# A state-space layer rewritten as a table of ticks, with every engine and the SP queue in program order

## The chip, the core and the metric

One core of a Trainium2 chip runs the kernel. The core has five instruction streams that matter here: PE (TensorE, matrix products), ACT (ScalarE, functions of one input), DVE (VectorE, element-wise work), POOL (GpSimd, element-wise work) and SP (SyncE, which here only issues DMAs). Each stream is executed in its own order, and streams wait for each other through semaphores. The metric is the device time of one execution in microseconds (us), lower is better.

## The reference

The function is one decode and prefill step of a two-layer model: a state-space layer (Mamba-2 style, "SSD") and then a latent-attention layer ("MLA"). Only the SSD layer is touched. Cut to what matters:

```python
def ssd_mixer(h, conv_buf, ssm_state, w_in, conv_w, conv_b, dt_bias, a_log, d_skip, norm_w, w_out):
    proj = jnp.einsum('btd,de->bte', h, w_in)
    z, xbc, dt_raw = ...                                  # gates, inputs of the convolution, steps
    xbc, new_buf = causal_conv(xbc, conv_buf, conv_w, conv_b)
    xbc = jax.nn.silu(xbc)                                # x (32 heads x 64), B and C (8 groups x 128)
    dt = jax.nn.softplus(dt_raw + dt_bias)
    y, new_state = ssd_scan(x, dt, -jnp.exp(a_log), B, C, ssm_state)
    y = (y + d_skip * x) * jax.nn.silu(z)
    yg = y per group of 256 channels
    y = yg * lax.rsqrt(mean(yg * yg) + eps) * norm_w
    out = jnp.einsum('bte,ed->btd', y, w_out)
```

There are 1024 prompt tokens and 8 sample sequences of 8 tokens, 1088 rows in all. The scan works on chunks of 128 tokens. With `a` the running sum of the decays in a chunk, one chunk needs M = exp(a_l - a_s) * (C B^T) below the diagonal, y = M (x dt) + exp(a) C S, and the state S = fade * S + (x dt decay)^T B. The samples start from states in memory, and return new ones.

## The kernel before

**Precision and tiling.** A product in full precision is done as three products of halves: every factor is split into a rounded part (hi) and the rest (lo), and `mm3` or `mm_tok` add hi*hi, hi*lo and lo*hi in one PSUM bank. A split (`split`, L127) is a copy on ACT (hi) and a subtraction on DVE or POOL (lo). The 1088 rows are nine tiles, the last one (64 rows) is the samples.

**Groups.** The layer goes through eight groups of four heads. A group has two parts. The *projections* (class `Group`): four blocks of 128 channels (B, C, and two of x), each in three column pieces of 384, 384 and 320 tokens (products named pj, 24 a piece); each piece is copied out of PSUM by ACT into `raw`, then the convolution is one ACT operation and three DVE operations (`acc`, L468) of 1112 columns; and nine tiles of gates (products named pz, 24 a tile). The weights come in pieces of 256 KB (`wraw`, L272), which ACT and DVE split into `wih` and `wil`. The *scan* (`ssd_scan`): for each of nine tiles PE transposes x and B (trp), makes C B^T (cb), the product within the chunk (py), the state's increment (st) and the product with the state (py from Sh, Sl); DVE, ACT and POOL make what these need. The ninth tile is the samples: four pieces of old state (s) are loaded, transposed (s0p), split (sh, sl), used (pv) and renewed (sn, s).

**What sets the order.** The code is written as generators: the loop over groups in `layer_ssd` runs the projections of group g+1 beside the scan of group g, by weights, and a scheduler then orders each engine's instructions by its own model, so neighbours in the code need not be neighbours on an engine. The scheduler also pulls weights of group 1 ahead into the time of group 0 (seven 256 KB pieces).

**Ahead of the loop** stand group 0's projections and `ssd_dt` (L335), which turns the step sizes into decays: ACT, DVE and PE work on `dtu`, `acs`, `acsp`, and then SP writes the decays to memory (`acs_d`, L387) and copies `tok` (L376, six small DMAs). The scan reads `acs_d` back once for each chunk (M, L573).

**After the loop** comes the output projection, in two halves of eight input blocks (`ssd_outproj`, products poa and pob): `load_wout` loads and splits w_out (woh L703, wol L704), each tile of y is read back, scaled, transposed (ytp), split and multiplied. The first half runs beside the scan of group 7. The MLA layer follows.

The change and the prediction touch L575 (four DVE operations a chunk that make min(a_l - a_s, 0) for M), L577 (exp on ACT), L578 (times C B^T), L656 to L664 (y, the gate, the square for the norm, the multiplication by the norm weight nw on POOL, the store), L477 (co: the last three columns of the convolution on their way out, from the PSUM bank ctp), L129 and L130 (the two halves of a split) and L429 (silu of the convolution).

Of the kernel before, what the change touches and what calls it, by code (L numbers as in the profile page):

```python
# [8 lines left out]
F32 = mybir.dt.float32  # L9
# [7 lines left out]
D = 1024  # L17
# [62 lines left out]
PB1 = {"tr": 2, "pj": 2, "cb": 1, "y": 2, "st": 1}  # L80
# [254 lines left out]
def ssd_dt(k, pool, psum):  # L335
# [19 lines left out]
    pt = psum.tile([128, 512], F32, tag="y", name="dpt", bufs=PB["y"])  # L355
# [50 lines left out]
class Group:  # L406
# [10 lines left out]
    def pair(self, pi, both=False):  # L417
# [3 lines left out]
        if both:  # L421
            for _ in range(3):
# [6 lines left out]
        nc.scalar.activation(acc[:, :, :SEQ], acc[:, :, :SEQ], AF.Silu)  # L429
        nc.scalar.activation(xs.rearrange("p a (b w) -> p a b w", w=NT),  # L430
                             bass_window(acc, SEQ + 3, NT + 3, NT), AF.Silu)
        self.xc.append((acc, xs))
        if pi:
            self.conv_out()
# [53 lines left out]
    def gates(self):  # L488
# [4 lines left out]
        for i, (t0, m) in enumerate(TILES):  # L493
# [15 lines left out]
            if i == 4:  # L509
                nc.scalar.activation(z, z, AF.Silu)  # L510
            yield
# [9 lines left out]
def ssd_scan(k, gr, pools):  # L521
    nc, I = k.nc, k.I
    sp, psum = pools
    g = gr.g
    S = None
    hs = slice(4 * g, 4 * g + 4)
    nw = sp.tile([128, 256], F32, tag="nw", name=f"nw{g}", bufs=1)
    nc.sync.dma_start(nw, I["ssd_norm_w"][0, 256 * g : 256 * g + 256].partition_broadcast(128))
    for i in ORDER[g]:
        t0, m = TILES[i]  # L530
        sl = slice(t0, t0 + m)
        smp = i == 8
        B, C, X0, X1 = (gr.xc[q][1][:, j] if smp else gr.xc[q][0][:, j, sl] for q in range(2) for j in range(2))
        z = gr.z[i // 5][:m, i % 5]
        tag = f"{g}_{i}"
        p = psum.tile([128, 512], F32, tag="tr", name="trp" + tag, bufs=PB["tr"])
        nc.tensor.transpose(p[:m, 0:128], X0, k.ident)
        nc.tensor.transpose(p[:m, 128:256], X1, k.ident)
        if not smp:
            nc.tensor.transpose(p[:m, 256:384], B, k.ident)  # L540
        xsT = sp.tile([128, 256], F32, tag="xsT", name="xsT" + tag, bufs=2)
        nc.scalar.copy(xsT[:m], p[:m, 0:256])
        if not smp:
            Bh, Bl = (sp.tile([128, 128], F32R, tag="BT" + x, name="BT" + x + tag, bufs=2) for x in "hl")
            split(k, Bh, Bl, p[:, 256:384])
        tk = k.tok[:m, i]

        def hb(j):
            return tk[:, j, hs].unsqueeze(2).to_broadcast([m, 4, 64])

        def v3(t):
            return t[:m].rearrange("p (h q) -> p h q", q=64)

        xdt = sp.tile([128, 256], F32, tag="xdt", name="xdt" + tag, bufs=2)
        nc.vector.tensor_tensor(v3(xdt), v3(p[:, 0:256]), hb(1), op=ALU.mult)  # L555
        if not smp:
            xdd = sp.tile([128, 256], F32, tag="xdd", name="xdd" + tag, bufs=1)
            nc.gpsimd.tensor_tensor(v3(xdd), v3(xsT), hb(2), op=ALU.mult)
            dh, dl = (sp.tile([128, 256], F32R, tag="xdd" + x, name="xdd" + x + tag, bufs=1) for x in "hl")
            split(k, dh, dl, xdd, nc.gpsimd)  # L560
            if S is not None:
                Ch, Cl = (sp.tile([128, 128], F32R, tag="C" + x, name="C" + x + tag, bufs=1) for x in "hl")
                split(k, Ch, Cl, C, nc.gpsimd)
                Sh, Sl = (sp.tile([128, 256], F32R, tag="S" + x, name="S" + x + tag, bufs=1) for x in "hl")
                split(k, Sh, Sl, S, nc.gpsimd)
# [30 lines left out]
        else:  # L596
# [7 lines left out]
            for q in range(2):  # L604
# [20 lines left out]
                for pr in range(2):  # L625
# [4 lines left out]
                    for b in range(4):  # L630
                        nc.tensor.transpose(pt[:, b * 128 : b * 128 + 128], s0[:, b], k.ident)
# [1261 lines left out]
```

## Time and profile before

| | us |
|---|---|
| time, median of 3 runs | 2100.28 (2096.88 to 2101.25) |
| the profiled execution, first to last instruction (its span) | 2095.4 |
| loop over groups 1 to 7 (first pj of group 1 to last pz), from 116.7 | 730.9 |
| rest of the scan and first half of the output projection | 169.0 |
| second half of the output projection | 106.9 |
| MLA layer, from 1123.5 | 971.9 |

The profile has no time of its own for the profiled execution beside its span; the median run is 4.9 us longer than that span, which is what lies around it.

A page of the profile lists the busy time of each engine, then groups of instructions (line, engine, operation, written tile <- read tiles, count, busy time, mean of one, idle time ahead of it and what ended that). The view by windows gives for one stretch of time: start and end, length, then busy time and count of PE, PE's weight loads, DVE, ACT and POOL, then the clock that PE was granted (1.00 is full), the share of the DMA engines and GB/s. The timeline gives start, duration, engine, line, operation, tiles and, in brackets, how long the engine had been idle and for whom.

### The profile page before, as it was taken

Reading aid. Unit: us, or ns where it says so; the run is one execution under the profiler, and the core shown is the slowest. Engines: PE = TensorE matmul, PEld = TensorE weight load, DVE = VectorE, ACT = ScalarE, POOL = GpSimd, SP = SyncE. Lnnn points to the kernel's source line nnn. Section 1 sums busy time; section 2 is a strip of 40 time slices with the busy share of each in tenths; the row PEclk is TensorE's granted clock in tenths of the full one; section 3 lists DMA queues with packets and bytes.
Section 4 is the critical chain, followed back from the end, with each engine's and each line's share of the span. In section 5 each row is a group of like instructions: output and inputs, shape, how many; then the busy total and the mean of one; then the engine's idle time right before and its main releaser. Section 6 shows DMA issues by size and latency. Waiting matters only on the chain.

```text
span 2095.4 us, 33766 instructions
## 1 busy us (share of the span) xinstructions
PE 1948.3 (93%) x12001; PEld 1763.6 (84%) x12001; DVE 1340.1 (64%) x2838; ACT 1043.3 (50%) x2287; POOL 851.9 (41%) x1059
## 2 busy tenths in 40 slices
PE   6999999999999999789998999699999999889998
PEld 5898999899999998677787998698888888778887
DVE  4558676767676767865334314366787778776665
ACT  5455565556565656522114323234676667755552
POOL 0337564646664646744000001102343334765541
PEclk9999999999999999889999999899999989999999
DMA  4222324231324241635534342132111112464451
GB/s 144 56 59 64 111 66 115 56 114 57 105 66 115 56 115 46 208 122 192 183 124 133 124 152 63 52 108 68 48 55 52 43 37 61 133 197 131 142 152 40
DMA packets 187631, 207.61 MB, mean 99 GB/s; under 512 B 23260, under 2 KB 153064, under 8 KB 187080
## 3 DMA queue, kind: packets, MB, share of 16 engines
q1 hardware_dynamic: 182408, 185.67, 29.2%
q0 software_dynamic: 4976, 19.66, 3.0%
q8 instruction: 95, 1.56, 0.3%
q14 instruction: 72, 0.59, 0.1%
q10 hardware_dynamic: 80, 0.13, 0.0%
HBM read 152.10 MB, written 53.28 MB: 98 GB/s over the span
## 4 chain that ended last, share of the span: by engine, by line
PE 33%; DVE 9%; issue 4%; POOL 4%; DMA 3%; ACT 2%; SPq 0%; POOLq 0%; DVEq 0%; ACTq 0%
PE pq L100 5%; PE pob L100 5%; PE pj L88 4%; PE poa L100 2%; POOL kvl L1541 2%; PE pk L100 1%; PE p L100 1%; PE vp L88 1%; PE st L1246 1%; DVE tl L1260 1%; PE st L1248 1%; PE st L1247 1%; PE o L1277 1%; PE sc L1214 1%; PE kp L88 1%
## 5 line engine op out<-in xcount | busy, mean ns | idle before, releaser
L88 PE MATMUL pj<-xh,wih 128*128 128x384 f32 (+1 forms) x768 | 254.9, 336 | 10.9 <-ACT xh L235 6.6
L88 PE MATMUL pj<-xl,wih 128*128 128x384 f32 (+1 forms) x768 | 255.9, 333 | 0.0
L88 PE MATMUL pj<-xh,wil 128*128 128x384 f32 (+1 forms) x768 | 255.1, 332 | 0.0
L1260 POOL TENSOR_TENSOR tl<-P,th 128x384 fp32r<-128x384 f32 (+1 forms) x96 | 90.7, 945 | 181.0 <-ACT P L1258 138.5
L88 PEld LDWEIGHTS pj<-xh,wih 128*128 128x128 f32 x768 | 145.8, 191 | 12.5 <-ACT xh L235 7.5
L468 DVE SCALAR_TENSOR_TENSOR acc<-raw,vec,acc 128x1112 f32<-128x1112 f32 x96 | 147.0, 1535 | 11.9 <-ACT acc L465 11.1
L88 PEld LDWEIGHTS pj<-xh,wil 128*128 128x128 f32 x768 | 146.3, 190 | 0.6
L88 PEld LDWEIGHTS pj<-xl,wih 128*128 128x128 f32 x768 | 146.1, 190 | 0.5
L575 DVE TENSOR_SCALAR M<-M,tok 128x128 f32<-128x128 f32 (+1 forms) x288 | 116.6, 462 | 43.0 <-DMA M<-acs_d 35.7
L100 PE MATMUL pz<-wih,xh 128*128 128x256 f32 x504 | 143.0, 287 | 0.0
L100 PE MATMUL pz<-wil,xh 128*128 128x256 f32 (+1 forms) x504 | 142.8, 287 | 0.0
L1257 ACT ACTIVATE th<-st 128x512 fp32r<-128x512 f32 x192 | 94.1, 490 | 73.6 <-PE st L1253 54.7
L100 PE MATMUL pz<-wih,xl 128*128 128x256 f32 x448 | 128.1, 286 | 0.0
L130 DVE TENSOR_TENSOR wil<-wraw,wih 128x512 fp32r<-128x512 f32 x88 | 70.4, 802 | 65.7 <-ACT wih L129 63.1
L1541 POOL TENSOR_TENSOR kvl<-pgr,kvh 128x1024 fp32r<-128x1024 f32 x32 | 78.2, 2445 | 67.8 <-ACT kvh L1540 67.8
L100 PEld LDWEIGHTS pz<-wih,xh 128*128 128x128 f32 x504 | 96.0, 190 | 1.1
L577 ACT ACTIVATE M<-M 128x512 f32<-128x512 f32 (+1 forms) x72 | 43.8, 608 | 102.0 <-DVE M L575 101.7
L1258 ACT ACTIVATE P<-st 128x512 f32<-128x512 f32 x192 | 93.2, 486 | 0.0
L100 PEld LDWEIGHTS pz<-wil,xh 128*128 128x128 f32 (+1 forms) x504 | 92.9, 184 | 0.3
L663 POOL TENSOR_TENSOR y<-y,nw 128x256 f32<-128x256 f32 (+1 forms) x72 | 64.5, 896 | 70.2 <-ACT xD L662 69.7
L582 PEld LDWEIGHTS py<-xdt,M 128*128 128x128 f32 (+1 forms) x576 | 70.4, 192 | 19.8 <-DVE xdt L555 6.5
L100 PEld LDWEIGHTS pz<-wih,xl 128*128 128x128 f32 x448 | 85.4, 191 | 0.4
(819 smaller groups left out, 6461.6 us busy)
## 6 DMA issues: line engine op xcount, KB each, us to landing
wraw<-in_ssd_w_in SPq DMA_DIRECT2D x92, 256.0 KB
M<-acs_d SPq DMA_DIRECT2D x64, 256.0 KB
s<-in_state_ssm SPq DMA_DIRECT2D x32, 256.0 KB
y_d<-y SPq DMA_DIRECT2D x64, 128.0 KB
out_s_ssm<-s SPq DMA_DIRECT2D x32, 256.0 KB
wraw<-in_ssd_w_out SPq DMA_DIRECT2D x16, 512.0 KB
q_d<-qt SPq DMA_DIRECT2D x32, 192.0 KB
qp<-q_d SPq DMA_DIRECT2D x8, 768.0 KB
```

The source lines that it names most:

```text
L88: nc.tensor.matmul(out, a, b, start=(i == 0), stop=(i == n - 1))
L100: nc.tensor.matmul(o, a, b, start=(j == 0), stop=(j == len(ops) - 1))
L130: (eng or nc.vector).tensor_tensor(lo, src, hi.bitcast(F32), op=ALU.subtract)
L468: nc.vector.scalar_tensor_tensor(acc, raw[:, j : j + n], k.convw[j][:, blk : blk + 1], acc, op0=ALU.mult, op1=ALU.add)
L575: nc.vector.tensor_scalar(M[:m, h, :m], M[:m, h, :m], tk[:, 0, 4 * g + h : 4 * g + h + 1], 0.0, op0=ALU.subtract, op1=ALU.min)
L577: nc.scalar.activation(M[:m, :, :m], M[:m, :, :m], AF.Exp)
L582: nc.tensor.matmul(py[:m, h * 64 : h * 64 + 64], M[:m, h, :m], xdt[:m, h * 64 : h * 64 + 64], start=True, stop=True)
L663: nc.gpsimd.tensor_tensor(y[:m], y[:m], nw[:m], op=ALU.mult)
L1257: nc.scalar.activation(th[:, :n], ps[:, :n], AF.Exp, scale=SCALE)
L1258: nc.scalar.activation(P[:, :n], ps[:, :n], AF.Exp, scale=SCALE)
L1260: eng.tensor_tensor(tl[:, :n], P[:, :n], th[:, :n].bitcast(F32), op=ALU.subtract)
L1541: nc.gpsimd.tensor_tensor(rl, raw, rh.bitcast(F32), op=ALU.subtract)
```

## The change

From the end of group 0's projections to the end of the output projection the order is now written by hand. `layer_ssd` opens a block in which the five streams PE, ACT, DVE, POOL and SP keep the order of the code, and calls `ssd_groups`. `Flow` holds the projections of group g, `Scan` the scan of group g-1, `OutProj` and `WOut` the output projection. A group is 21 ticks: 12 pieces of pj, then 9 tiles of pz. In each tick PE first gets the tick's projection, then the other engines get the element-wise work of the scan (`scan.ew`) and of the projections (`fl.ew`), loads and splits of weights, the copy of the projection out of PSUM as ACT's last operation (`ev`), and PE gets its part of the scan (`scan.pe`) behind its projection. Scan tile i has its transposes in tick 2i-2 (`front`), its element-wise work in ticks 2i-1 (`front1`) and 2i (`front2`, `decayed`), its products in tick 2i+1 (`back`), its y in ticks 2i+2 and 2i+3 (`out1`, `out2`). The samples' states are transposed in ticks 12, 14, 16, 18 and used in 13, 15, 17, 19. After group 7's projections the table goes on for 47 ticks: ticks 0 to 8 hold only the scan of group 7 and the splits of w_out, ticks 9 to 26 the first half of the output projection (beside the rest of the scan), ticks 27 to 44 the second half.

Some arithmetic changes too. min(a_l - a_s, 0) is made by four ACT operations (Relu with a bias and scale -1, then exp with scale -1) in place of four on DVE. The multiplication of y by nw on POOL is gone, with its DMA; the norm weight is multiplied into w_out while it is split (ACT copy with a scale, and one DVE operation with a scale for all sixteen blocks, where POOL did half of them). The PSUM bank of y is single, pv has a bank of its own, and sn uses the bank of cb. s has three buffers for two. Group 0's projections and the MLA layer keep their instructions; in group 0 the silu of the first two blocks and the copy co stand a little later.

```diff
-PB1 = {"tr": 2, "pj": 2, "cb": 1, "y": 2, "st": 1}
+PB1 = {"tr": 2, "pj": 2, "cb": 1, "y": 1, "pv": 1, "st": 1}
...
+    def split(self, p):
+        raw = self.raws.pop(p)
+        shape = [128, 4, 128] if p < 8 else [128, 2, 256]
+        hi, lo = (self.wp.tile(shape, F32R, tag="wi" + x, name="wi" + x, bufs=WB) for x in "hl")
+        split(self.k, hi, lo, raw)
+        self.parts[p] = kslices((hi, lo), shape[1])
...
+    def ew(self, t):
+        k, g, nc = self.k, self.g, self.k.nc
+        if t < 9 and t % 3:
+            p = 2 * (t // 3) + 1 + t % 3
+            self.split(p)
+            self.load(p + 2)
+        if t in (9, 10):
+            self.split(t - 1)
+            self.load(t + 1)
+        if t == 11:
+            self.split(10)
...
+        if t in (16, 17):
+            acc, xs = self.xc[t - 16]
+            nc.scalar.activation(acc[:, :, :SEQ], acc[:, :, :SEQ], AF.Silu)
+            nc.scalar.activation(xs.rearrange("p a (b w) -> p a b w", w=NT),
+                                 bass_window(acc, SEQ + 3, NT + 3, NT), AF.Silu)
+        if t == 14:
+            self.co = self.rp.tile([128, RAW], F32, tag="raw", name=f"co{g}", bufs=2)[:27, :512]
+            nc.vector.tensor_copy(self.co, self.ctp[:27])
...
+        if t == 13:
+            self.ctp = self.psum.tile([128, 512], F32, tag="tr", name=f"ctp{self.g}", bufs=PB["tr"])
+            for bi in range(4):
+                self.k.nc.tensor.transpose(self.ctp[:27, bi * 128 : bi * 128 + 128], self.ct[:, bi], self.k.ident)
...
-            nc.vector.tensor_scalar(M[:m, h, :m], M[:m, h, :m], tk[:, 0, 4 * g + h : 4 * g + h + 1], 0.0,
-                                    op0=ALU.subtract, op1=ALU.min)
+            nc.scalar.activation(M[:m, h, :m], M[:m, h, :m], AF.Relu, bias=c.tk[:, 0, 4 * g + h : 4 * g + h + 1], scale=-1.0)
-        nc.scalar.activation(M[:m, :, :m], M[:m, :, :m], AF.Exp)
+        nc.scalar.activation(M[:m, :, :m], M[:m, :, :m], AF.Exp, scale=-1.0)
...
+class Scan:
...
+    def ew(self, t):
+        if t in (10, 11, 12):
+            self.load_state(t - 10)
+        if t in (15, 17, 19, 21):
+            n = (t - 15) // 2
+            nc.sync.dma_start(self.state_rows(k.O["s_ssm"], n), self.s0[n])
+        if t == 17:
+            self.load_state(3)
+        if not odd:
+            if t < 16:
+                self.load_decay(i + 1)
+            if t in (14, 16, 18, 20):
+                self.add_state((t - 14) // 2)
+            if i == 0:
+                self.front1(0)
+            if i < 8:
+                self.decayed(i)
+            if 1 <= i <= 8:
+                self.state(i - 1)
+            if i <= 8:
+                self.front2(i)
+            if 1 <= i <= 8:
+                c = self.c[i - 1]
+                self.out1(c, c.py, c.py[:, 256:] if i > 1 else None)
+        else:
+            if t in (13, 15, 17, 19):
+                self.split_state((t - 13) // 2)
+            if i < 8:
+                self.fade(i)
+                self.front1(i + 1)
+            if 1 <= i <= 8:
+                self.out2(self.c[i - 1])
...
+    def pe(self, t):
+        if not odd and i < 8:
+            self.front(i + 1)
+        if odd and i < 8:
+            self.back(i)
+        if t in (10, 15):
+            self.turn_copies(t == 15)
+        if t in (12, 14, 16, 18):
+            self.turn_state((t - 12) // 2)
+        if t in (13, 15, 17, 19):
+            self.use_state((t - 13) // 2)
...
-        nc.gpsimd.tensor_tensor(y[:m], y[:m], nw[:m], op=ALU.mult)
+    def split(self, kk, pool=None):
+        nc, raw = self.k.nc, self.raw.pop(kk)
+        hi, lo = ((pool or self.pool).tile([128, D], F32R, name=f"wo{x}{kk}") for x in "hl")
+        nw = self.k.ssdn[:, kk : kk + 1]
+        nc.scalar.activation(hi, raw, AF.Copy, scale=nw)
+        nc.vector.scalar_tensor_tensor(lo, raw, nw, hi.bitcast(F32), op0=ALU.mult, op1=ALU.subtract)
...
+def ssd_groups(k, g0, pools, sp, psum, st, left, right):
+    tc, nc = k.tc, k.nc
+    gr, pscan = g0, None
+    scan = Scan(k, g0, (sp, psum))
+    scan.ew(-1)
+    scan.pe(-1)
+    nxt = Flow(k, 1, pools)
+    for p in range(2):
+        nxt.load(p)
+    for p in range(2):
+        nxt.split(p)
+        nxt.load(p + 2)
+    for g in range(1, G):
+        fl, nxt = nxt, Flow(k, g + 1, pools) if g < G - 1 else None
+        for t in range(21):
+            ev = fl.proj(t)
+            if t == 0 and pscan:
+                gr.ew(21)
+                pscan.ew(21)
+            scan.ew(t)
+            fl.ew(t)
+            if nxt and t == 11:
+                nxt.load(0)
+            if nxt and t == 19:
+                nxt.split(0)
+                nxt.load(2)
+            fl.late(t)
+            if nxt and t == 11:
+                nxt.load(1)
+            if nxt and t == 20:
+                nxt.split(1)
+                nxt.load(3)
+            ev()
+            scan.pe(t)
+            fl.pe(t)
+        pscan, scan, gr = scan, Scan(k, fl, (sp, psum)), fl
+        scan.ew(-1)
+        scan.pe(-1)
...
+    for t in range(B0 + 20):
+        ev = None
+        for o, T in ((oa, A0), (ob, B0)):
+            u = t - T
+            if o and 0 <= u < 18:
+                ev = o.proj(*divmod(u, 2))
+        if t == 0:
+            gr.ew(21)
+            pscan.ew(21)
+        if t < 8:
+            scan.ew(t)
+            wsa.append(wo.split(t))
+            wo.load(t + 2)
+        elif t < 22:
+            scan.ew(t)
+        if t == 4:
+            oa = OutProj(k, (ya,) * 9, wsa, psum, 0, x_loader(k), "a")
+        if t in (9, 10):
...
+        with tc.manual_schedule(engines={e.engine for e in (nc.tensor, nc.vector, nc.scalar, nc.gpsimd, nc.sync)}):
+            ssd_groups(k, g0, pools, sp, psum, st, left, right)
```

How the rows move, at the three places that matter below. A row is a line number, an operation, the written tile <- the read tiles, and a shape.

**SP at the end of group 0, before.** The rows are the DMAs that SP issues; L272 are weights, L328 and L329 the last weights of group 0, L480 the first of the convolution's outputs.

```order
L338 DMA blks<-in_c_blks 64x128
L272 DMA wraw<-in_ssd_w_in 128x4x128 x3
L328 DMA wraw<-in_ssd_w_in 128x4x256
L329 DMA wraw<-in_ssd_w_in 128x4x32
L272 DMA wraw<-in_ssd_w_in 128x4x128 x4
L480 DMA out_p_conv<-co_784 3x128
```

All seven L272 loads here are group 1's, ahead of the decays (acs_d comes eight rows further down). The same place in the change, from the last output of the convolution on:

```order
L481 DMA out_s_conv<-co_839 24x256
L387 DMA acs_d<-acsT 128x2x128
L388 DMA acss_d<-acsT 32x64
L376 DMA tok_76<-tok 32x32 x6
L672 DMA M_0_1098<-acs_d 128x512
L541 DMA wraw<-in_ssd_w_in 128x4x128 x4
L672 DMA M_1_1149<-acs_d 128x512
L541 DMA wraw<-in_ssd_w_in 128x4x128
```

The first weights of group 1 (L541) now stand behind acs_d, acss_d, six tok and the first M.

**DVE in the last part of group 1's scan, ticks 13 and 14 of the change.** The first row closes tick 13, the next seven are tick 14, the last opens tick 15. L853 renews a piece of state, L757 adds to S, L723 makes M, L769 and L770 y, L617 is the convolution, L631 copies the bank ctp out.

```order
L617 SCALAR_TENSOR_TENSOR acc_1752<-raw_1691,vec,acc_1752 128x1112
L853 TENSOR_TENSOR s_1796<-s_1796,sn_2070 128x512
L757 TENSOR_TENSOR S_7_2022<-S_7_2022,st_6_2049 128x256
L723 TENSOR_TENSOR M_7_1955<-M_7_1955,cbm_7_2034 128x512
L769 TENSOR_TENSOR y_6_2118<-py_6_2050,tok 128x256
L770 TENSOR_TENSOR y_6_2118<-y_6_2118,py_6_2050 128x256
L617 SCALAR_TENSOR_TENSOR acc_1752<-raw_1691,vec,acc_1752 128x1112
L631 COPY co_2127<-ctp_2072 27x512
L130 TENSOR_TENSOR sl_2167<-s0p_2135,sh_2166 128x512
```

The place of the same copy before:

```order
L468 SCALAR_TENSOR_TENSOR acc_1541<-raw_1780,vec,acc_1541 128x1112
L594 TENSOR_TENSOR S_7_1883<-S_7_1883,st_6_1879 128x256
L656 TENSOR_TENSOR y_6_1889<-py_6_1874,tok 128x256
L477 COPY co_1939<-ctp_1934 27x512
L468 SCALAR_TENSOR_TENSOR acc_1541<-raw_1780,vec,acc_1541 128x1112
```

Co now stands behind a state's renewal, M, both y and the last convolution operation of the tick. On PE the bank ctp is wanted again in the same tick, by the second s0p.

**ACT in ticks 16 and 17 of the change.** L719 is exp of M, L799 and L806 are the samples' b3 and x3, L626 and L627 the silu of the first two blocks, L586 the copy of a gate tile out of PSUM, L129 sh the split of a piece of state.

```order
L719 ACTIVATE M_8_2102<-M_8_2102 64x4x64
L799 CAST b30True<-x3p0True 96x128
L806 CAST x30True<-xf0True 96x256
L626 ACT_TABLE_LOAD
L626 ACTIVATE acc_1353<-acc_1353 128x2x1024
L627 ACTIVATE xs_1354<-acc_1353 128x128
L586 COPY z_1924<-pj_16_2219 128x256
L129 CAST sh_2301<-s0p_2267 128x512
L779 ACTIVATE y_7_2250,yssq<-xD_7_2115 128x256
```

Before, the split of the first piece of state stood so:

```order
L616 CAST x_80_2160<-xf_80_2158 96x256
L619 CAST b_80_2163<-x3p_80_2150 96x128
L129 CAST sh_800_2175<-s0p_800_2170 128x512
L508 COPY z_1971<-pz 128x256
L510 ACTIVATE z_1971<-z_1971 128x1280
```

In the change the third piece's split (sh) stands behind a function-table load, the silu of 2048 columns, and a copy that waits for PE.

More of the change, by code (lines that the diff above doesn't have):

```diff
@@ L530, in ssd_scan @@
         t0, m = TILES[i]
+        smp = i == 8
         sl = slice(t0, t0 + m)
[L532 to L540 removed]
@@ L541, in ssd_scan @@
[L541 to L554, printed above, removed]
```

604 lines of the change are left out of this document (405 added, 199 removed).

## The prediction

> **What bounds the kernel now.** I read the page's busy line first, then the view by windows.
>
> ```profile
> PE 1948.3 (93%) x12001; PEld 1763.6 (84%) x12001; DVE 1340.1 (64%) x2838; ACT 1043.3 (50%) x2287; POOL 851.9 (41%) x1059
> 116.70:847.60 730.90, 702.37 (x5047) 676.71 (x5045) 529.33 (x1052) 415.50 (x936) 430.52 (x637) 0.99 0.30 84
> 742.50:847.60 105.10, 100.39 (x729) 96.59 (x727) 77.70 (x151) 59.31 (x135) 59.12 (x88) 1.00 0.28 81
> 847.60:1016.60 169.00, 147.05 (x733) 118.64 (x732) 110.99 (x180) 53.31 (x118) 82.97 (x86) 0.91 0.53 174
> 1016.60:1123.50 106.90, 104.49 (x483) 83.76 (x484) 34.73 (x49) 14.78 (x28) 1.69 (x3) 1.00 0.40 133
> 1123.50:2095.40 971.90, 900.56 (x5160) 797.27 (x5158) 614.22 (x1491) 507.72 (x1115) 313.40 (x286) 0.96 0.31 95
> ```
>
> PE bounds it: in the loop of groups 1 to 7 it is busy 702 of 731 us, 104.4 us a group (730.9/7). The change touches the stretch from 116.7 to 1123.5; the last 971.9 us keep their instructions. What can be won in the loop is what PE wastes there, so I compare 104.4 us with PE's dense time. Starts of successive products, from the timeline:
>
> ```profile
> 240.22 0.28 PE L88 MATMUL st<-xddl,BTh 128*128 128x256 f32 x1
> 240.34 0.28 PE L88 MATMUL st<-xddh,BTl 128*128 128x256 f32 x1
> 240.46 0.34 PE L88 MATMUL pj<-xh,wil 128*128 128x384 f32 x1
> 240.63 0.34 PE L88 MATMUL pj<-xh,wih 128*128 128x384 f32 x1
> ...
> 243.49 1.00 PE L582 MATMUL py<-xdt,M 128*128 128x64 f32 x8
> 244.30 0.37 PE L88 MATMUL st<-xddh,BTh 128*128 128x256 f32 x1
> ...
> 248.65 0.27 PE L537 MATMUL trp<-ident,acc 128*128 128x128 f32 x1
> 248.76 0.27 PE L538 MATMUL trp<-ident,acc 128*128 128x128 f32 x1
> ...
> 250.66 0.31 PE L88 MATMUL pj<-xh,wih 128*128 128x320 f32 x1
> 250.81 0.30 PE L88 MATMUL pj<-xl,wih 128*128 128x320 f32 x1
> ```
>
> A duration here is pipelined (0.34 us), the step from start to start is the cost: 0.174 us for 384 columns, 0.147 for 320, 0.12 for 256, 0.11 for a transpose, 0.9 for the eight passes of py with what they delay. A group has 4 blocks x 24 x (0.174 + 0.174 + 0.147) = 47.5 us of pj, 8 x 24 x 0.12 + 16 x 0.12 = 25.0 of pz, and in the scan 26 trp (2.8), 8.5 times py (7.7), 24 st and 21 state products (45 x 0.12 = 5.4), nine cb in two passes (2.0), and about 6 for the samples' pieces (estimated at the same steps). Sum 96.4 (the steps quoted for st stand for all of 256 columns). So 8.0 us of each group are waits. Where they are:
>
> ```profile
> PE st L88 <- ACT xddh L129: 10.6, 13, 1.8
> PE py L582 <- DVE xdt L555: 5.2, 6, 1.6
> ```
>
> These are waits of PE at the entry of scan work (us in seven groups, times, longest); with the smaller rows they make the 28.5 us in which PE is seen idle, 4.1 a group, and the rest of the 8 hides behind the modelled ends. Scan inputs come too late because the order puts them just ahead of their use.
>
> **Part 1, the start of the loop (a loss).** Before, PE starts pj of group 1 at 116.7, while the chain of decays runs:
>
> ```profile
> 129.92 0.42 DVE L383 COPY acsT<-acsp 128x256 f32<-128x256 f32 x1 [1.97 <-PE acsp L381]
> 127.97 4.09 SPq L376 DMA_DIRECT2D tok<-tok  x6
> 132.17 0.52 SPq L387 DMA_DIRECT2D acs_d<-acsT  x1
> 133.30 0.94 SPq L272 DMA_DIRECT2D wraw<-in_ssd_w_in  x2
> 224.37 0.37 SPq L272 DMA_DIRECT2D wraw<-in_ssd_w_in  x1
> 227.37 0.62 ACT L129 CAST wih<-wraw 128x512 fp32r<-128x512 f32 x1 [2.35 <-DMA wraw<-in_ssd_w_in]
> ```
>
> By the order of the change the first weights are issued behind acs_d, acss_d, six tok and M. With PE free, acsT is ready about 127; acs_d and acss_d take 0.9, tok 4.1 (the row above), M 0.5: weights at 132.8. Landing takes 3.0 (224.37 to 227.37), the split's first half 0.6, and the first pj starts at 136.7 instead of 116.7. Nothing covers this: no other products are ready. **Loss 20.0 us.** In PE's idle time the clock falls:
>
> ```profile
> 1342.00:1348.00 6.00, 0.00 (x0) 0.00 (x0) 0.00 (x0) 0.00 (x0) 0.00 (x0) 0.50 0.19 41
> 1353.00:1356.00 3.00, 3.00 (x12) 2.86 (x12) 2.15 (x10) 2.50 (x8) 0.54 (x1) 0.53 0.18 66
> ```
>
> After an idle stretch PE worked 3 us at 0.53 of its clock, so another 1.6 us go. [...]
>
> **Part 2, seven groups (a gain).** In the table PE's scan work stands a whole tick (4.2 us with pj, 2.9 with pz) behind what it needs, so most of the 8 us can go. I walked through 21 ticks with these durations:
>
> ```profile
> L468 DVE SCALAR_TENSOR_TENSOR acc<-raw,vec,acc x96: 1354/1377/2939, 60.4 to 821.7; 128x1112 f32<-128x1112 f32 x96
> L575 DVE TENSOR_SCALAR M<-M,tok 128x128 f32<-128x128 f32 (+1 forms) x260 | 99.1, 439 | 42.9 <-DMA M<-acs_d 35.7 <-DMA M<-acss_d 7.1
> L578 DVE TENSOR_TENSOR M<-M,cbm 128x512 f32<-128x512 f32 (+1 forms) x63 | 47.3, 751 | 15.0 <-ACT M L577 13.7
> L130 DVE TENSOR_TENSOR sl<-s0p,sh 128x512 fp32r<-128x512 f32 x27 | 18.6, 689 | 5.1 <-ACT sh L129 4.7
> L663 POOL TENSOR_TENSOR y<-y,nw 128x256 f32<-128x256 f32 (+1 forms) x62 | 54.5, 880 | 65.0 <-ACT xD L662 64.9
> L129 ACT CAST BTh<-trp 128x128 fp32r<-128x128 f32 x56 | 15.6, 279 | 1.3 <-PE st L88 1.3
> L429 ACT ACTIVATE acc<-acc 128x2048 f32<-128x2048 f32 x14 | 26.8, 1915 | 9.1 <-DVE acc L468 9.0
> L577 ACT ACT_TABLE_LOAD x20 | 25.7, 1283 | 1.7 <-DMA M<-acs_d 1.3
> L129 ACT CAST sh<-s0p 128x512 fp32r<-128x512 f32 x27 | 15.6, 579 | 3.0 <-PE s0p L631 2.9
> ```
>
> The arithmetic edits: DVE loses 36 operations of 0.44 (16 us a group); ACT gains 36 Relu, of which the trace has none. Nothing is a gain, so the low end is 0; the high end is 0.44, DVE's for the same tile; I take 0.28, the ACT operation on 128x128: 10 us a group. ACT was busy 59 of 105 us and saves table loads, since silu now stands in ticks 16 to 18 only (two loads of 1.28 a group where the loop had about six). It stays near 65 of 101, beside PE. POOL loses nine multiplications of 0.88, 8 us a group. All of this is off the critical path: worth nothing by itself, it only gives slack. A PE wait remains in two ticks:
>
> - **Tick 14.** The second s0p needs the bank that ctp holds until co is copied, DVE's last operation of the tick. From the end of tick 13 on PE, DVE does the state's renewal and S (1.1), waits for ACT's Sh and exp (to about 2.2), then M 0.75, two y 0.83, L617 1.4, co 0.67: 5.9. PE does its pz (2.9) and trp and cb (0.5): 3.4. Wait 2.5.
> - **Tick 17.** The third piece of state needs sh and sl, and ACT does sh behind tick 16's x3 (3.4 after the tick's start, behind DVE's xf), table load 1.28, silu 1.92, its small part 0.3 and the gate copy 0.37: 7.3; then sh 0.58, sl 0.69: 8.6. PE gets there at 2.9 + 0.4 + 2.9 = 6.2. Wait 2.4.
>
> I add 0.1 for small ones, since all others have a tick of slack: 96.4 + 2.5 + 2.4 + 0.1 = **101.4 us a group**, so the loop's last pz ends at 116.7 + 20.0 + 1.6 + 7 x 101.4 = 848.1, against 847.6. Start and loop nearly cancel.
>
> **Part 3, the tail (a gain).** Before it takes 169.0 + 106.9 = 275.9 us from the last pz, and the first half of the output projection has a clock of 0.91.
>
> ```profile
> 868.32 0.33 SPq L702 DMA_DIRECT2D wraw<-in_ssd_w_out  x1
> 873.74 1.04 ACT L703 CAST woh<-wraw 128x1024 fp32r<-128x1024 f32 x1 [0.76 <-DMA wraw<-in_ssd_w_out]
> 1039.71 0.39 PE L100 MATMUL pob<-woh,yhb 128*128 128x512 f32 x1
> 1039.94 0.39 PE L100 MATMUL pob<-wol,yhb 128*128 128x512 f32 x1
> L204 POOL TENSOR_TENSOR yrsb<-yrsb,nhalf 128x36 f32<-128x36 f32 x1 | 6.1, 6139 | 1.9 <-DVE yrsb L199 1.9
> ```
>
> Ticks 0 to 8 have no projection, so PE idles through them. One of the two w_out buffers goes round in landing 5.0, hi 1.04, lo 1.4 (unseen; bounded by 0.75 for DVE's 512 columns and 2.4 for POOL's 1024, I take the convolution's L468), issue 0.4: 7.8 us for two ticks. Nine ticks make 35, the first landing 5, the power on POOL (6.1) delays by some 3: tick 9 starts 43 us after the last pz. Then 16 half tiles of 24 products of 0.23 and two of 16 make 95.7 us, with transposes 8, less those done in ticks 7 and 8 (3), the rest of group 7's scan on PE (about 14), and some 5 of waits: 120. The second half, 106.9 now, holds 95.7 + 8 of work; with the tick of slack I take 103. Sum 43 + 120 + 103 = 266: **gain 10 us**, with some 8 us either way.
>
> **Sum.** +20.0 + 1.6 - 7 x 3.0 - 10 = -9.4 (104.4 - 101.4 = 3.0), against the profiled execution: 2086.0, and with the 4.9 us around the span **2091** beside the median of 2100.3.
>
> **The rivals.**
> 1. *The two ticks don't wait.* For it: DVE loses a third of its scan work and may be ahead in tick 14, and s0p may find the other bank free. Against it: the rows in order. Then a group is 97.4 (96.4 and 1.0 of small waits), the loop 28 us shorter: 2063.
> 2. *Gains and losses cancel.* PE's hidden waits stay as small gaps, a group takes 102.7, 1.3 more: 2100. For it: half of the 8 us isn't seen as idle time, and some may be no wait.
> 3. *DVE in program order is late, and PE waits every group (slower).* Place: ticks 11 to 14, where DVE has to do 5.7, 4.2, 3.6 and 4.7 us in ticks of 5.1, 3.9, 5.5 and 3.9 at L617's median. The L468 row goes to 2.94 for the same tile. If POOL's work beside it stretches four of these operations by 0.8 each (half of the 1.56 between median and maximum), 3.2 us go to PE at tick 14: a group takes 104.6, the time is 2113. It decides from 1.9 us more a group (103.3). Against it: POOL's 0.88 multiplications go, and before DVE was busier (77.7 of 105). [...]
>
> That the change doesn't hold the order it writes is excluded by the order's rows.
>
> **How the numbers follow.** Forecast 0.42, rival 1 0.18, rival 2 0.14, rival 3 0.26. A measurement of this kernel can tell about 0.2% (4 us) from no change. Faster: the forecast but for its slowest part and rival 1, 0.58; same 0.16; slower 0.26. The forecast's own range, by the tail's 8 us, is 2083 to 2099. For 8 in 10 I reach to rival 1 and rival 3: 2062 to 2116, which takes in a Relu of 0.44 (ACT 6 us a group busier, still under PE).
>
> **What would show it.** First pj at 136 to 137, with weights waited for; seven group lengths near 101; in each a wait of PE at s0p for DVE's co and one at pv for sl of 2 to 3 us; the first poa near 891. Wrong would be group lengths over 103, PE waiting for M, st's or py's inputs, or for ACT's copies out of PSUM in pz ticks, and a tail longer than 276.

## The result, and the profile after

| | before | after |
|---|---|---|
| time, median of 4 runs each on the same chip | 2098.58 us | 2188.30 us |
| range of the runs | 2092.17 to 2101.25 | 2184.56 to 2196.72 |
| ratio | | 1.0428, 95% interval 1.0394 to 1.0462 |
| span of the profiled execution | 2095.4 us | 2190.1 us |
| start of the first pj of group 1 | 116.70 us | 138.38 us |
| loop of groups 1 to 7, first pj to last pz, a seventh of it | 104.2 us | 112.9 us |
| from the last pz to the output projection's last pob | 277.3 us | 287.3 us |

The change makes the kernel 4.3% slower, 90 us. The forecast was 9 us faster, and the time lies far outside its range. The profile of before has the last pz end at 846.09 and the last pob at 1123.43; the marks 847.6 and 1123.5 of the table ahead of the prediction are a little later. By the ends of these products the spans' difference of 94.7 us splits so: the start has 21.7 of it, the loop 60.6 (790.0 for 729.4), the tail 10.0, and MLA 2.4. (MLA's first pj of after starts 4.8 us behind the last pob, of before 1.6: its weights land later, and ACT waits 5.50 us for them at 1218.98.)

The windows show (length, then busy time of PE, PEld, DVE, ACT and POOL with their instructions, the granted clock of PE, the DMA share, GB/s), first two of before, the loop and MLA, then those of after, in order: the gap ahead of the loop; the loop; group 3's ticks with pj; its ticks with gate tiles, 12 to 20; the tail up to the first poa; the output projection's first half; its second half; MLA.

```profile
116.70:846.09 729.39, 701.58 (x5041) 676.03 (x5039) 528.49 (x1050) 414.40 (x934) 430.47 (x636) 0.99 0.30 84
1123.43:2095.40 971.97, 900.63 (x5160) 797.34 (x5158) 614.25 (x1491) 507.72 (x1115) 313.40 (x286) 0.96 0.31 95
117.00:138.40 21.40, 6.56 (x21) 4.29 (x21) 3.29 (x9) 7.85 (x12) 1.64 (x4) 0.54 0.16 46
138.38:928.40 790.02, 731.62 (x5044) 710.94 (x5045) 448.22 (x787) 443.10 (x1148) 406.40 (x572) 0.94 0.27 78
365.49:427.34 61.85, 61.46 (x405) 60.33 (x404) 36.15 (x65) 36.89 (x101) 36.61 (x56) 1.00 0.30 89
427.34:478.18 50.84, 43.03 (x321) 41.18 (x320) 27.97 (x50) 27.01 (x67) 21.49 (x27) 0.87 0.23 65
928.40:978.77 50.37, 22.93 (x92) 18.77 (x90) 28.07 (x51) 29.59 (x70) 33.59 (x32) 0.53 0.47 152
978.77:1114.00 135.23, 123.40 (x628) 101.95 (x628) 65.69 (x107) 36.72 (x87) 32.98 (x39) 0.96 0.48 153
1114.00:1215.72 101.72, 101.72 (x483) 83.62 (x482) 37.01 (x50) 14.19 (x26) 0.90 (x2) 1.00 0.45 145
1215.72:2190.10 974.38, 902.73 (x5161) 798.07 (x5158) 614.45 (x1490) 507.34 (x1115) 312.13 (x285) 0.96 0.31 95
```

PE has as many instructions in the loop as before (5044 and 5041), DVE has 263 fewer, and no engine but PE is busy for more than 57% of the loop. The loss sits in one part of each group. The 12 ticks with pj run dense: 61.5 busy of 61.9 us, clock 1.00. The nine gate ticks show PE idle for 7.8 us and a mean clock of 0.87. The waits of PE in this one group (us in total, times, longest):

```profile
PE s0p L826 <- DVE co L631: 1.9, 1, 1.9
PE pj L100 <- ACT wih L129: 1.9, 1, 1.9
PE pj L100 <- DVE wil L130: 1.8, 2, 1.4
PE pv L847 <- ACT sh L129: 1.7, 1, 1.7
PE pv L847 <- DVE sl L130: 0.5, 1, 0.5
```

With a row of 0.3 these are 8.1 us. Against the prediction's dense 96.4, group 3 (112.7 us) reads as 96.4 + 8.1 of waits + (1 - 0.87) x 50.8 = 6.6 lost to the clock + 1.6 that no row names. (Some 0.5 of the clock's 6.6 falls while PE waits at tick 12, so about 2.1 is unnamed.) Two of these terms were not in the forecast: the weights' wait at tick 12 (1.9 and 1.8), and the clock.

Tick 14 of group 2 shows how a wait and the clock go together. First PE in the timeline, then DVE, then windows of 3.41 us:

```profile
336.70 0.66 PE L826 MATMUL s0p<-ident,s 128*128 128x128 f32 x4 [1.93 <-DVE co L631]
```

```profile
333.19 0.80 DVE L723 TENSOR_TENSOR M<-M,cbm 128x512 f32<-128x512 f32 x1 [1.08 <-ACT M L719]
333.91 0.41 DVE L769 TENSOR_TENSOR y<-py,tok 128x256 f32<-128x256 f32 x1
334.35 0.42 DVE L770 TENSOR_TENSOR y<-y,py 128x256 f32<-128x256 f32 x1
334.69 1.37 DVE L617 SCALAR_TENSOR_TENSOR acc<-raw,vec,acc 128x1112 f32<-128x1112 f32 x1
335.98 0.67 DVE L631 COPY co<-ctp 27x512 f32<-27x512 f32 x1
```

```profile
333.93:337.35 3.42, 1.49 (x14) 1.15 (x13) 2.69 (x5) 0.37 (x1) 2.93 (x5) 1.00 0.00 0
337.35:340.76 3.41, 3.41 (x19) 3.41 (x18) 1.48 (x4) 2.32 (x8) 1.62 (x2) 0.50 0.12 42
340.76:344.17 3.41, 3.41 (x34) 3.41 (x34) 0.00 (x0) 0.95 (x3) 0.61 (x1) 1.00 0.09 20
```

PE waits 1.93 us while DVE, behind M and two y, goes through L617 and the copy. The clock is still 1.00 during this wait. It falls when PE is at work again: 3.41 us at 0.50, so 1.7 us of work are lost. PE counts as busy there, so a list of waits shows only about half of the price.

At tick 12 the wait is for the weights of the first gate tile. ACT's timeline, then DVE's, then PE's:

```profile
317.12 0.40 ACT L806 CAST x31False<-xf1False 96x256 fp32r<-96x256 f32 x1 [0.80 <-DVE xf1False L802]
317.43 1.14 ACT L129 CAST wih<-wraw 128x512 fp32r<-128x512 f32 x2
```

```profile
317.56 0.42 DVE L807 TENSOR_TENSOR x31False<-xf1False,x31False 32x256 fp32r<-32x256 f32 x1 [0.47 <-ACT x31False L806]
318.08 0.69 DVE L130 TENSOR_TENSOR wil<-wraw,wih 128x512 fp32r<-128x512 f32 x1
318.68 1.37 DVE L617 SCALAR_TENSOR_TENSOR acc<-raw,vec,acc 128x1112 f32<-128x1112 f32 x1
319.97 1.22 DVE L130 TENSOR_TENSOR wil<-wraw,wih 128x512 fp32r<-128x512 f32 x1
```

```profile
318.10 0.39 PE L100 MATMUL pj<-wih,xh 128*128 128x256 f32 x1 [1.93 <-ACT wih L129]
```

```profile
321.24 0.58 PE L100 MATMUL pj<-wil,xh 128*128 128x256 f32 x1 [1.44 <-DVE wil L130]
```

The split of the weights stands last in tick 11, behind the samples' triples, in which ACT waits for DVE (0.80) and DVE for ACT (0.47) in turn. An L617 stands between the low parts of the two pieces. Over the loop neither engine is near its limit; what is late here is this chain of small mutual waits and the operation in between.

### The profile page after: what moved, and what is told of

Read it like the earlier page. It is cut to its first block, busy times and chain, and to the rows that moved or that the text cites. A ratio compares the mean times of both kernels' runs of the same rounds, so it can differ in the third digit from the quotient of the medians.

```text
span 2190.1 us, 33508 instructions
## 1 busy us (share of the span) xinstructions
PE 1983.4 (91%) x12001; PEld 1805.7 (82%) x12001; DVE 1245.8 (57%) x2558; ACT 1089.8 (50%) x2547; POOL 809.8 (37%) x977
## 4 chain that ended last, share of the span: by engine, by line
PE 57%; DVE 17%; ACT 8%; issue 7%; DMA 5%; POOL 4%; SPq 1%; POOLq 0%; ACTq 0%; DVEq 0%
PE pj L88 16%; PE pq L100 5%; PE pj L100 5%; PE poa L100 5%; PE pob L100 4%; PE py L734 2%; DVE acc L617 1%; DVE tl L1632 1%; PE pk L100 1%; PE pz L100 1%; POOL kvl L1913 1%; DVE sc L1591 1%; DVE wil L130 1%; PE p L100 1%; PE vp L88 1%
## 5 line engine op out<-in xcount | busy, mean ns | idle before, releaser
L100 PE MATMUL pj<-wih,xh 128*128 128x256 f32 x504 | 158.9, 319 | 13.5 <-ACT wih L129 13.5
L100 PE MATMUL pj<-wil,xh 128*128 128x256 f32 (+1 forms) x504 | 155.1, 314 | 11.8 <-DVE wil L130 11.8
L617 DVE SCALAR_TENSOR_TENSOR acc<-raw,vec,acc 128x1112 f32<-128x1112 f32 x84 | 134.8, 1605 | 40.0 <-ACT acc L613 40.0
L100 PE MATMUL pj<-wih,xl 128*128 128x256 f32 x448 | 139.7, 312 | 0.0
L100 PEld LDWEIGHTS pj<-wih,xh 128*128 128x128 f32 x504 | 110.8, 220 | 14.9 <-ACT wih L129 14.9
L100 PEld LDWEIGHTS pj<-wil,xh 128*128 128x128 f32 (+1 forms) x504 | 107.8, 214 | 15.3 <-DVE wil L130 14.7
L771 POOL TENSOR_TENSOR y<-y,xD 128x256 f32<-128x256 f32 x64 | 82.1, 1284 | 102.5 <-DVE y L770 102.2
L723 DVE TENSOR_TENSOR M<-M,cbm 128x512 f32<-128x512 f32 (+1 forms) x72 | 54.3, 755 | 91.7 <-ACT M L719 91.7
L100 PEld LDWEIGHTS pj<-wih,xl 128*128 128x128 f32 x448 | 100.2, 224 | 0.0
L130 POOL TENSOR_TENSOR xddl<-xdd,xddh 128x256 fp32r<-128x256 f32 x64 | 69.2, 1081 | 83.3 <-ACT xddh L129 82.6
L710 ACT ACTIVATE M<-M,tok 128x128 f32<-128x128 f32 (+1 forms) x288 | 90.5, 388 | 12.6 <-DMA M<-acs_d 12.5
```

Source lines behind the costliest of these rows:

```text
L100: nc.tensor.matmul(o, a, b, start=(j == 0), stop=(j == len(ops) - 1))
L130: (eng or nc.vector).tensor_tensor(lo, src, hi.bitcast(F32), op=ALU.subtract)
L617: nc.vector.scalar_tensor_tensor(acc, raw[:, j : j + n], k.convw[j][:, blk : blk + 1], acc, op0=ALU.mult, op1=ALU.add)
L710: nc.scalar.activation(M[:m, h, :m], M[:m, h, :m], AF.Relu, bias=c.tk[:, 0, 4 * g + h : 4 * g + h + 1], scale=-1.0)
L723: nc.vector.tensor_tensor(M[:m, :, :m], M[:m, :, :m], c.cbm[:m, :m].unsqueeze(1).to_broadcast([m, 4, m]), op=ALU.mult)
L771: nc.gpsimd.tensor_tensor(y[:m], y[:m], c.xD[:m], op=ALU.add)
```

## The experiments

A group is, below, the mean length from the first pj of group 1 to that of group 7, a sixth of it; after has 112.9, before 104.3. The first eight kernels (e_swap to e_pre) ran on one chip, on which the kernel before took 2099.6 us beside the first four and 2088.8 beside the next four; e_four, e_pre2 and e_best ran on another, with 2094.3. All but e_best2 ran once, and the kernel before differs by up to 10 us between these; so what follows goes by the starts of the groups in the traces, with the times beside them.

**e_swap: xdt behind the split of B.** At tick 11 ACT's BTh waits 2.65 us for DVE's xdt, which reads the same bank ahead of it; the theory was that this wait makes the weights late.

```diff
@@ front1
-        xdt = c.xdt = self.tile([128, 256], "xdt", "xdt" + tag, 2)
-        nc.vector.tensor_tensor(c.v3(xdt), c.v3(p[:, 0:256]), c.hb(1), op=ALU.mult)
         if not smp:
...
             nc.gpsimd.tensor_tensor(c.v3(c.xdd), c.v3(xsT), c.hb(2), op=ALU.mult)
+        xdt = c.xdt = self.tile([128, 256], "xdt", "xdt" + tag, 2)
+        nc.vector.tensor_tensor(c.v3(xdt), c.v3(p[:, 0:256]), c.hb(1), op=ALU.mult)
```

> In each odd tick ACT's BTh waits 2.65 us for DVE's xdt, which is written ahead of it and reads the same PSUM bank; here xdt is written behind the split of B, so that ACT waits no longer. Theory (ACT's late wih in tick 11 makes PE wait 3.7 us in tick 12, and the clock halves after it, 3.2 us more): a group falls from 112.7 to 106 to 108, the time by 35 to 45 us, to about 2148. Rival (the weights' landing, or DVE's wil behind the convolution, makes that wait): a group stays above 111, the time above 2175.

2189.0 us, 112.3 a group. The theory falls: ACT's wait for xdt is gone and the wait at tick 12 stays at 1.6 and 1.8, since ACT then waits 1.91 us for PE ahead of its split of C in the same tick.

**e_co: the copy of co as DVE's first operation of tick 14.**

```diff
+            if t == 14:
+                fl.out_conv()
             scan.ew(t)
```

(out_conv holds the two lines of the copy, taken out of the convolution's part of the tick.)

> The copy co is DVE's first operation of tick 14 in place of its last. Theory (the wait of 1.9 us, and the half clock behind it, 1.7 us): a group falls by 3.6, the time by 25 us, to 2163. Rival A (only the wait counts, the clock would have fallen anyhow): a group falls by 1.9, the time by 13. Rival B (the next late input takes the wait's place): no change.

2163.9 us, 109.6 a group: 3.4 less for a wait of 1.9, which is gone from the profile. The theory's sum was 1.9 + 1.7.

**e_silu: the first two silu one tick later, behind the split of sh, and the gate's silu at tick 20.**

```diff
-        if t in (16, 17):
-            acc, xs = self.xc[t - 16]
+        if t in (17, 18):
+            acc, xs = self.xc[t - 17]
...
-        if t == 18:
+        if t == 20:
             nc.scalar.activation(self.z[0], self.z[0], AF.Silu)
```

> The two silu of the convolution move from ticks 16 and 17 to 17 and 18, behind the split of the third state; the silu of the first five gate tiles moves from tick 18 to 20. Theory (the wait of 2.2 us in tick 17 and the half clock behind it, 1.7 us): a group falls by 3.9, the time by 27 us, to 2161. Rival A (only the wait counts): 2.2 a group, 15 us. Rival B (the next late input, or the silu ahead of the next group's transposes, takes its place): no change.

2167.1 us, 109.6 a group: 3.4 less, where the wait was 2.2 and 3.9 were expected; PE's wait for sh is gone, that of 0.5 for sl stays. So the causes named for ticks 14 and 17 were right, and each costs 1.5 to 1.8 times its wait.

**e_warm: repeated products ahead of the gate tiles of ticks 12, 14 and 17,** to tell waits from the clock. They keep PE at work while it would wait; the products that follow overwrite them.

```diff
+        n = {12: 28, 14: 14, 17: 16}.get(t, 0)
+        for j in range(n):
+            nc.tensor.matmul(p[:m, :256], k.xh[:, 0, TILES[i][0] : TILES[i][0] + m], ws[0][0], start=j == 0, stop=j == n - 1)
         drain(mm_tok(nc, p, m, 256, [(*both(k.xh, k.xl, i, kk), *ws[kk]) for kk in range(8)]))
```

> As the changed kernel, with 28, 14 and 16 products of 256 columns, whose result is overwritten, ahead of the gate tiles of ticks 12, 14 and 17, so that PE works (3.4, 1.7 and 1.9 us) where it waited. Theory (a wait of about 2 us lowers the clock for some 5 us after it): the waits shrink by what is filled in, the clock stays at 1.00 in the gate ticks, a group falls by 5 to 6.6, to 106 to 108, the time by 35 to 46 us, although PE does more work. Rival (the clock falls for another reason, or the waits only move): a group stays at 112 to 114, the time at 2188 or above.

2173.8 us, 111.1 a group. The gate ticks of groups 2 and 3 by windows, the second of them the same ticks as in the row of after above:

```profile
312.29:361.19 48.90, 45.13 (x379) 43.92 (x378) 28.09 (x50) 26.76 (x67) 21.52 (x27) 0.97 0.24 69
422.98:470.45 47.47, 43.70 (x379) 42.50 (x378) 28.08 (x50) 26.85 (x67) 21.51 (x27) 1.00 0.24 70
```

PE does 58 products more in the nine ticks, and these take 47.5 to 48.9 us instead of 50.8, at a clock of 0.97 to 1.00 instead of 0.87. More work in less time: so the clock is a cost by itself. The size expected was missed (111.1 for 106 to 108): the wait for co stayed behind the products put ahead of it, at 2.4 us.

**e_wei: the splits of the gate weights 3 and 4 ahead of the scan's work in tick 11,** the triples behind them.

```diff
+            if t == 11:
+                fl.split(10)
             scan.ew(t)
+            if t == 11:
+                fl.split(11)
+                scan.triples(0)
             fl.ew(t)
```

> In tick 11 the split of the gates' third weight piece stands ahead of all scan work, and that of the fourth ahead of the samples' triples (b3, xf, x3), in place of behind them. Theory (the ping-pong of ACT and DVE over the triples, not BTh's wait, made the gate weights late): PE's waits for wih and wil in tick 12 fall from 3.7 to under 1 us, the clock stays at 1.00 there (3.2 us), a group falls from 112.7 to about 106.5, the time by 43 us, to 2145. Rival (the landing of the weights binds): under 1.5 us a group, 10 us.

2188.6 us, 113.0 a group: no gain. Waits of PE in the stretch of group 3 (360 to 470 us):

```profile
PE py L731 <- DVE y L767: 1.8, 1, 1.8
PE pv L844 <- ACT sh L129: 1.7, 1, 1.7
PE s0p L823 <- DVE co L629: 1.6, 1, 1.6
PE pv L844 <- DVE sl L130: 0.7, 2, 0.5
PE sn L846 <- POOL ct L614: 0.6, 1, 0.6
PE pj L100 <- ACT wih L129: 0.5, 1, 0.5
PE pj L100 <- DVE wil L130: 0.3, 1, 0.3
```

The wait for the weights falls from 3.7 us to 0.8, so their place in tick 11 was what made them late. In its place PE's py waits 1.8 for y, which empties py's only bank: in group 2 that y starts at 324.64, 0.7 us later than in after (323.96), and PE, which the weights no longer hold, is there before it. In sum PE's waits in group 3 are 7.5 us for 8.1.

**e_three: e_wei, e_co and e_silu together.**

> The edits of e_wei, e_co and e_silu together. Theory (three waits and the half clock behind each, 7.9 and 6.6 us, add up): a group is 98 to 100, the clock in the gate ticks 1.00, the time 2188 - 95 = 2093, no slower than the kernel before. Rival (once these are gone the next late input of DVE or ACT makes PE wait): a group stays above 104, the time above 2125.

2150.8 us, 106.2 a group, so the rival held. The waits for co and sh are gone as in the single kernels, and what e_co and e_silu gained alone (3.4 and 3.4) makes up all of the 6.7 gained here. The third part, e_wei's, adds nothing: py's wait for y (1.8) stays, with the clock at 0.92 in the gate ticks of group 2 and at 1.00 in those of group 3.

**e_relu: the Relu back on DVE,** the rest as after.

```diff
-            nc.scalar.activation(M[:m, h, :m], M[:m, h, :m], AF.Relu, bias=c.tk[:, 0, 4 * g + h : 4 * g + h + 1], scale=-1.0)
+            nc.vector.tensor_scalar(M[:m, h, :m], M[:m, h, :m], c.tk[:, 0, 4 * g + h : 4 * g + h + 1], 0.0,
+                                    op0=ALU.subtract, op1=ALU.min)
```

> The changed kernel with min(a_l - a_s, 0) on DVE again (four operations a scan tile; exp without its scale). Theory (the move to ACT is worth only slack): DVE gets 36 x 0.44 = 16 us a group, most in odd ticks, so the waits for wil and co grow by 0.5 to 2 us each: a group rises by 1 to 4 us, the time to 2195 to 2215. Rival (ACT with its Relu is what is late): a group falls, the time to 2150 to 2175.

2204.9 us, 115.1 a group. This part of the change is worth 2.2 us a group as the order stands: with the Relu on DVE, PE's waits in group 3 for co and for wih grow from 1.9 to 3.1 and 2.9, so DVE's load is not free in these ticks.

**e_pre: four pieces of group 1's first weights loaded, and two of them split, ahead of the decays.**

> The first four weight pieces of group 1 are loaded, and two of them split, ahead of the decays, in the part that the scheduler orders. Theory (weights behind the decays on SP make the gap at the start): the first pj of group 1, now at 138.4, starts at about 127 to 130, behind the decays' small products and the first scan tile on PE, since these keep the order of the code; the time falls by 9 to 12 us, to 2177. Rival (the order on PE alone, decays first, makes the gap): it starts at 135 or later, under 4 us.

2177.4 us; the first pj at 129.8 instead of 138.4, group 2 at 242.4 instead of 252.9, and the groups as long as in after (112.7). The start is a loss of its own and adds to the others.

**e_pre2: in addition the projections of ticks 0 to 2 of group 1 ahead of the decays.**

> As e_pre, and the first block's three pieces of group 1 (ticks 0 to 2) are multiplied ahead of the decays, where the scheduler orders; nothing else moves. Theory (PE has nothing to do while the decays run): PE works from 117 on, the loop ends 20 to 23 us earlier than in the changed kernel, the time is 2166. Rival (what is moved ahead is missing in ticks 0 to 2, where ACT and DVE then make PE wait): 11 us as with e_pre, 2177.

2181.2 us, no gain over e_pre: group 2 begins at 246.5 us, 4.1 later than in e_pre. Rows of SP, ACT and PE in the timeline of e_pre2:

```profile
131.85 3.97 SPq L376 DMA_DIRECT2D tok<-tok  x6
136.27 0.83 SPq L672 DMA_DIRECT2D M<-acs_d  x2
140.01 1.28 ACT L710 ACTIVATE M<-M,tok 128x128 f32<-128x128 f32 x4 [7.16 <-DMA M<-acs_d]
141.63 0.58 PE L88 MATMUL st<-xddh,BTh 128*128 128x256 f32 x1 [7.72 <-ACT xddh L129]
```

With the projections earlier, the first scan step's M is what is late: it stands behind six small transfers on SP, ACT waits 7.2 us for it, and ACT's next split keeps PE for 7.7.

**e_four: e_three and e_swap, the first triple spread over ticks 6, 7 and 9, and exp and M of a chunk ahead of the state's addition in even ticks.**

```diff
-        if t in (9, 14):
+        if t in (6, 14):
             self.copies(t == 14)
-        if t in (11, 16):
+        if t in (9, 16):
             self.triples(t == 16)
```

> The edits of e_three and e_swap, with the samples' first triple three ticks earlier (ticks 6, 7 and 9 for 9, 10 and 11) and, in even ticks, exp and M ahead of the state's addition, so that DVE's M doesn't wait 1.06 us for ACT's Sh each time. Theory (in ticks 11 to 13 DVE and ACT wait for each other in program order, so that one late input takes the place of another, as wil and then y did): with this chain shortened by 2 to 4 us the rest goes too, a group falls from 106.3 to 98 to 101, the clock in the gate ticks is 1.00, the time is 2095 to 2115. Rival (DVE is simply full in these ticks): a group stays at 104 to 106, the time at 2135 to 2150.

2121.6 us, 103.1 a group, 9.8 less than after, between the theory's range and the rival's. Group 3 as a whole, its gate ticks, and PE's largest waits in it:

```profile
345.67:448.59 102.92, 98.68 (x725) 96.10 (x723) 66.91 (x114) 62.12 (x166) 58.59 (x82) 1.00 0.29 86
407.68:448.59 40.91, 37.36 (x322) 35.62 (x320) 28.74 (x49) 23.36 (x60) 23.67 (x29) 1.00 0.31 90
```

```profile
PE pj L100 <- ACT wih L129: 1.4, 1, 1.4
PE pv L845 <- DVE sl L130: 1.1, 2, 0.8
```

The gate ticks take 40.9 us instead of 50.8. No wait is over 1.4 us and the clock is 1.00. The loop's loss is therefore in the places where the order puts DVE's and ACT's work, not in that a table orders it.

**e_best: e_four and e_pre2, and the power of the output projection moved from the tail to tick 18 of group 7.**

> e_four and e_pre2 together, and the power for the first half's norm stands in tick 18 of group 7 in place of tick 4 of the tail. Sum of the parts: 2188 - 7 x 12.5 - 21 - 6 = 2074, faster than the kernel before by 0.5 to 1.5%. Rival (parts don't add, the tail's 16 us stay): 2090 to 2110.

2101.5 us, the rival's range; group 2 starts at 235.8 us (222.9 before), groups 2 to 6 take 102.9 each (103.9 before), and the tail 281.2, to the last pob.

**e_best2: in addition the six small transfers behind the first three M, and the w_out splits at ticks 9 and 10 of the tail later, at 15 and 17.**

> e_best with the six tok copies on SP behind the first three M (where they now stand 4 us ahead of the first one, for which PE waits 7.7 us at the first st), and the splits of the ninth and tenth block of w_out in ticks 15 and 17 of the tail in place of 9 and 10, where ACT and DVE wait for them. Theory (both are waits in program order that nothing hides): 4 to 7 us at the start and 3 to 8 in the tail, 2087 to 2095, faster than the kernel before by 0 to 0.5%. Rival (other inputs are as late): 2098 to 2102, the same as before.

The medians are 2103.9 us (ten runs) against 2098.3 for the kernel before beside it (thirteen); the ratio is given as 1.0014, interval 0.9991 to 1.0037, so no difference is shown. Group 2 begins at 233.0, 10.1 later than before, and the tail takes 276.4 (277.3 before). These steps take the loss back, and no kernel here beats the kernel before.

## Why the prediction was wrong, step by step

- **The bound: right; the dense time: too short.** PE bounds the kernel before and after. No run reaches the dense 96.4: in group 3 of e_four PE is busy 98.7 us at a clock of 1.00, 2.3 more, near the 2.1 that no row names above. With the late inputs moved a group comes to 103.1 from start to start (e_four), against 104.3 before. The gain sought in the loop exists, at 1.2 us a group instead of 3.0.
- **Part 1: right, 1.7 us short.** First pj at 138.4, forecast 136.7. The queue stood as foreseen; the six tok took 4.49 instead of 4.1. The clock stayed at 0.50 for the first 4.4 us of work, which costs 2.2 instead of 1.6. No run shows the 1.6: the row above it in the forecast, 3.00 us at 0.53, gives 1.4.
- **Part 2, the two waits: right.** 1.9 at tick 14 (forecast 2.5) and 2.2 at tick 17 (forecast 2.4), for co and for sh with sl. e_co and e_silu confirm both causes.
- **Part 2, "I add 0.1 for small ones, since all others have a tick of slack": this step failed.** The weights of the first gate tile were late by 3.7: their splits stand last in tick 11 and PE wants them at the start of tick 12, so they had no tick of slack. e_wei, which moves them, confirms the place. The walk counted each engine's durations, but not that ACT and DVE wait for each other within a tick. How common that is, one row shows: DVE, with fewer operations than before, stands idle for 81 us of the loop for ACT's exp alone.

```profile
L723 DVE TENSOR_TENSOR M<-M,cbm 128x512 f32<-128x512 f32 (+1 forms) x63 | 47.3, 751 | 81.0 <-ACT M L719 81.0
```

  Which share of these 81 us reaches PE, no run tells.
- **Part 2, the clock: this step failed too.** The half clock was counted once, at the start, and put at nothing in the groups, though a wait of about 2 us was forecast in two ticks of each. It costs 6.6 us a group in group 3. In tick 14 of group 2 a wait of 1.93 us was followed by 3.41 us at 0.50. By the rows of this case the forecast's two waits should have stood 1.7 higher each, and the group at 101.4 + 2 x 1.7 = 104.8, which is no gain.
- **Relu on ACT:** four took 1.28 us in a row, 0.32 each, for 0.28 taken. The edit gains 2.2 us a group (e_relu), where the prediction had "worth nothing by itself".
- **Rival 3 was nearest.** It had the place (DVE in program order, ticks 11 to 14) and the sign, not the mechanism or the size. L617 took 2.73 us at 327.79, while POOL ran s, S and xdd, but its least time, 1.37, in tick 14 at 334.69, where the rival put its price: there POOL's y (L771), which began later, took 1.79 us, against 0.73 at 234.19. No run took POOL's work away, so its share of the waits was not shown.
- **Part 3: wrong in sign, +10 instead of -10.** The first poa started 50.4 us after the last pz (forecast 43) and the first half took 135.2 (120): these two steps failed, by 7.4 and 15.2. The second half took 101.7 (103; 106.8 before) and was forecast rightly. The sum has no half clock where the first poa starts: the clock stayed at 0.50 for 3.70 us from there on, so 1.85 us were lost. The rows name these delays, of POOL, PE, PE and DVE:

```profile
955.95 6.15 POOL L204 TENSOR_TENSOR yrsa<-yrsa,nhalf 128x36 f32<-128x36 f32 x1
963.75 0.58 PE L88 MATMUL st<-xddh,BTh 128*128 128x256 f32 x1 [5.64 <-ACT xddh L129]
974.20 1.97 PE L998 MATMUL ytpa<-ident,yta 128*128 128x128 f32 x8 [4.84 <-DVE yta L988]
989.59 1.29 DVE L1054 SCALAR_TENSOR_TENSOR wol<-wraw,vec,woh 128x1024 fp32r<-128x1024 f32 x1 [8.82 <-ACT woh L1053]
```

  The w_out split's low half took 1.29, near the 1.4 taken; in these rows the tail's scan and projection wait for one another, for which the forecast had some 3 and 5 us. e_best2, with two of these places moved, has the tail at 276.4 and so takes the 10 us back, but with several edits at once: the shares are not told apart, and that stays open.

## What to carry to other kernels

In an order written by hand, walk ACT and DVE as one chain of waits on each other, not as two sums of durations per tick: a free engine is no slack if its next operation waits for the other. A short wait placed in a table comes back in every group, and its price is the wait and what the clock loses behind it (about 2 us of wait cost 3.4 us here). When one late input is moved, look at once for the next one: of two moves tried alone at tick 11, neither gained 1 us a group.

## What the runs showed of the hardware that was not expected

At tick 14 a wait of 1.9 us was followed by 3.41 us at a clock of 0.50, which began 0.65 us after the wait had ended. In the loop of after, from 142.79 us on, half clock comes in 20 stretches, 13 of 3.41 us and 7 of 6.83. It does not follow each such wait: in group 3 of e_three py waits 1.8 and the clock is 1.00, and before, waits at st reached 1.8 us with 0.99 over the loop. Rows of e_three, first two windows of 3.41 us from group 2, then two from group 3:

```profile
314.22:317.63 3.41, 1.62 (x14) 1.44 (x14) 2.29 (x5) 3.03 (x6) 2.15 (x3) 1.00 0.06 21
317.63:321.05 3.42, 3.42 (x20) 3.16 (x20) 3.09 (x7) 1.77 (x8) 3.42 (x5) 0.50 0.00 0
```

```profile
420.03:423.45 3.42, 1.71 (x15) 1.51 (x13) 2.31 (x7) 2.61 (x5) 1.97 (x3) 1.00 0.15 54
423.45:426.86 3.41, 2.43 (x20) 2.05 (x21) 3.08 (x7) 1.76 (x7) 3.39 (x5) 1.00 0.02 5
```

In group 2 PE is busy for 1.62 us of the first window, idle for 1.79, and the next one is at 0.50. In group 3, where py's wait for y is 1.79 us, PE is busy for 1.71 us of the first window, and the next one is at 1.00. So nearly the same idle time was followed by half clock in one group and not in the other; what decides it was not shown.

After's groups from the second on take 112.0 to 112.9 us and e_co's 109.2 to 109.3, about one stretch of 3.41 us less. Whether the length of these stretches has a part in the 3.4 us that e_co gained was not tested.
